# Nine pairs with seven products in the second column pair of the down projection, sums in used-up channels, and the pairs in another order

## The chip, the cores and the metric

The kernel runs on one core of a Trainium2 chip. The metric is the device time of one execution in microseconds; the number to predict is the median of several. The engines are PE (matmul), DVE (element by element), ACT (activation and casts), POOL, and SP, whose queue gives out the transfers (DMA). They run at once and wait for each other by semaphores. Each works through its own instructions in a fixed order.

## The reference

One decoder layer on 256 tokens and 16 meta tokens, width 2048: an attention group and a gated delta group side by side, an output projection, a residual, and then a SwiGLU FFN of width 5632. The change lies in the FFN, most of it in its last product:

```python
u = rmsnorm(h, ffn_norm_w[l])
h = h + (jax.nn.silu(u @ w_gate[l]) * (u @ w_up[l])) @ w_down[l]
```

Everything is float32, and the weights are read from memory once.

## The kernel before, in words

**Products in parts.** PE multiplies a faster 32-bit form with fewer bits. So each weight tile (2 x 128 rows by 512 columns, 512 KB, named raw) is split: ACT casts it to hi (L274), DVE takes lo = raw - hi (L275). The other operand is split too, and a product is three matmuls, hi by hi, lo by hi and hi by lo. A matmul makes 128 x 512 outputs in one of eight banks, two rings of four, mm and aux.

**The stream of weights.** Before anything runs, a list gives the weight tiles in the order of use (order) and the forms that they are split into (forms). Raw tiles have 4 buffers (WR), split ones 6 (WS and WS2). SP's queue issues the loads in the order of the list; a load into a buffer waits until DVE and ACT are done with the tile that was there, and what stands behind it in the queue waits too. next_w() hands out the next split tile and has those up to six further on split. The order of ACT and SP is that of the program. The order of DVE and PE is chosen by a scheduler when the program is built.

**Pairs with seven products.** The FFN's work is cut into pairs: two 128-channel rows of the weights (k, k+1) by two column tiles by two halves of the tokens (b), eight products of 128 x 128 by 128 x 512. A pair in SEVEN (the up and gate chunks) or DSEVEN (down) takes seven products instead, by sums of its four blocks. Its weights come as four forms: g (first column tile, as it is), u (half of the second), and t and s, sums of the two that DVE makes (L291 to L294). An ordinary pair has two forms, 24 matmuls and two lo on DVE; one with seven has four forms, 21 matmuls, and on DVE four sums of 512 columns, three lo of 1024 and one of 512. The sums of the other operand (the "sides", side_forms, L1318 to L1330, on DVE and ACT) are made once for each pair and serve both halves of down. The seven products go to four banks of the other ring as well (y), and are added up later (down_mid, L1500 to L1504).

**Order of the FFN.** Chunk 0 of gate and up, by stream() (L1199), then chunks 1 to 10 by block() (L1381), then down as two blocks, one for each pair of its four column tiles (p = 0 and 1). A block goes through its 22 pairs in the order 0, 1, ..., 21. Side work (evictions, side sums, splits of the hidden state) runs as tasks that advance a step at each product, so that they are written into the program between the matmuls. ffn_task (L1298) makes chunk 0's hidden state, in gact, and hands it after "yield 2" to to_hT, which transposes it on PE (L1277) into a bank of mm. The seven sides of down are made at the start of block p = 0, together with the splits of the last three chunks (whole, L1466 and L1468). At the start of p = 1, the outputs of p = 0 are summed (L1504, L1516) and written (L1518), and the residual x1 for the next two column tiles is fetched into the same buffers (fetch_x1, L1484).

Of the kernel before, what the change touches and what calls it, by code (L numbers as in the profile page):

```python
# [15 lines left out]
P = 128  # L16
D = 2048
KT = D // P
# [3 lines left out]
FFN = 5632  # L22
# [3 lines left out]
NCH = FFN // 512  # L26
# [5 lines left out]
WR, WS = 4, 4  # L32
WS2 = 2
WHOLE = 8
SEVEN = (2, 4, 6)
DSEVEN = (7, 9, 11, 13, 15, 17, 19)
PER_STEP = 2
SLOT = 4
WARM = 14
# [127 lines left out]
def layer(tc, xT, aw, x, w_in, w_ba, w_out, w_gate, w_up, w_down, cmask, dist, par, out):  # L167
# [21 lines left out]
    mm = Ring(mmp, "mm", 4, 512)  # L189
    tasks = Tasks(PER_STEP)  # L190
    aux = Ring(auxp, "aux", 4, 512, tasks.slot)
# [28 lines left out]
    wd_v = w_down.rearrange("(kt p) c -> p kt c", p=P)  # L220
    order = []
# [12 lines left out]
    def w_tile(wv, q, c):  # L234
        return wv[:, 2 * q:2 * q + 2, 512 * c:512 * (c + 1)], 2, 512
# [4 lines left out]
    forms = [("w", i) for i in range(len(order))]  # L240
    for c in range(1, NCH):
        for q in range(KT // 2):
            i = len(order)
            order += [w_tile(wv, q, c) for wv in (wg_v, wu_v)]
            forms += [("w", i), ("w", i + 1)] if q not in SEVEN else [("g", i), ("u", i), ("t", i), ("s", i)]
    for c in (0, 2):
        for q in range(FFN // P // 2):
            i = len(order)
            order += [w_tile(wd_v, q, c + j) for j in range(2)]
            forms += [("w", i), ("w", i + 1)] if q not in DSEVEN else [("g", i), ("u", i), ("t", i), ("s", i)]  # L250
    raws, ready, sums_ = {}, {}, {}

    pos = [0, 0, 0, 0]
# [127 lines left out]
    for k in range(KT):  # L381
        src, w = xr[k // 8][:, k % 8, :], aw_sb[:, k:k + 1]
# [870 lines left out]
    hT = {}  # L1253
# [18 lines left out]
    def to_hT(c, b, h_):  # L1272
# [7 lines left out]
        if c not in hT:  # L1280
# [3 lines left out]
            elif c < 7:  # L1284
                hT[c] = keep.tile([P, 2, 4, SEQ], F32R, tag=("v_c", "k_c", "q_c")[c - 4], name=n)
            elif c < WHOLE:
                hT[c] = fpool[0].tile([P, 2, 4, SEQ], F32R, tag=n, name=n)
            else:
                hT[c] = fpool[0].tile([P, 4, SEQ], F32, tag=n, name=n)
        bs = slice(P * b, P * (b + 1))  # L1290
        if c < WHOLE:
            S.copy(hT[c][:, 0, :, bs], pst)
# [6 lines left out]
    def ffn_task(c, b, pg, pu):  # L1299
        g_ = yield from fpool[1].get(512)  # L1300
        act(g_, pg, AF.Silu, scale=rr[:, b:b + 1])
        mm.free()
        yield at_least(f"up{c}", 1)
        yield 1
        ps = pu[b]
        V.scalar_tensor_tensor(g_, ps, rr[:, b:b + 1], g_, ALU.mult, ALU.mult)
        mm.free()
        yield 2
        yield from to_hT(c, b, g_)


# [2 lines left out]
    def side_forms(key, h, l, sh, sl):  # L1314

        v = yield from fpool[1].get(2, SEQ)
        w = yield from fpool[1].get(4, P)
        V.tensor_tensor(v, h, l, ALU.add)  # L1318
        a11, a21, a12, a22 = v[:, 0, 0:P], v[:, 0, P:SEQ], v[:, 1, 0:P], v[:, 1, P:SEQ]
        V.tensor_tensor(w[:, 0], a21, a22, ALU.add)  # L1320
        V.tensor_tensor(w[:, 1], w[:, 0], a11, ALU.subtract)
        V.tensor_tensor(w[:, 2], a11, a21, ALU.subtract)
        V.tensor_tensor(w[:, 3], a12, w[:, 1], ALU.subtract)
        yield 2
        h1, l1 = h[:, 0, P:SEQ], l[:, 0, P:SEQ]
        S.copy(h1, w[:, 0])
        S.copy(sh, w[:, 1:4])
        yield 1
        V.tensor_tensor(l1, w[:, 0], h1, ALU.subtract)
        V.tensor_tensor(sl, w[:, 1:4], sh, ALU.subtract)  # L1330
        fpool[1].free(2)
        sides[key] = [(h1, l1)] + [(sh[:, i], sl[:, i]) for i in range(3)]
        mark(f"side{key}")
# [30 lines left out]
        yield 10  # L1364
        yield from to_hT(c, b, h_)

    def block(c, name, nq, seven, lhs, need, mid, end):

        ring, other = rings[c % 2], rings[(c + 1) % 2]
        tasks.until(lambda: ring.live == 0)  # L1370
        x = [ring.now() for _ in range(4)]
        y = []
        n = nq - len(seven)
        left = {("x", i): 3 * (2 * n + (len(seven) if i < 3 else 0)) for i in range(4)}
        left.update({("y", i): 3 * len(seven) for i in range(4)})
        todo = dict(left)

        def product(bank, a, w):
            for l, r in ((a[0], w[0]), (a[0], w[1]), (a[1], w[0])):
                first, todo[bank] = todo[bank] == left[bank], todo[bank] - 1  # L1380
                PE.matmul((x if bank[0] == "x" else y)[bank[1]], l, r, start=first, stop=todo[bank] == 0)  # L1381

        for q in range(nq):
            k = 2 * q
            if need:
                tasks.until(need(k))
            if q not in seven:
                for col in range(2):
                    hi, lo = next_w()
                    for i in range(2):  # L1390
                        for b in range(2):
                            product(("x", 2 * col + b), lhs(k + i, b), (hi[:, i], lo[:, i]))
                            tasks.step()
                    if q == nq - 1:
                        end(col, x)
                continue
            if not y:
                tasks.until(lambda: other.live == 0)
                y += [other.now() for _ in range(4)]
            tasks.until(at_least(f"side{(name, q)}", 1))  # L1400
            s1, s2_, s3, s4 = sides[name, q]
            plan = (((("y", 0), lhs(k, 0), 0), (("x", 0), lhs(k + 1, 0), 1)), ((("x", 2), s4, 1),),
                    ((("y", 3), s1, 0), (("y", 2), s3, 1)), ((("y", 1), s2_, 0), (("x", 1), lhs(k + 1, 1), 1)))
            for part in plan:
                hi, lo = next_w()
                for bank, a, i in part:
                    product(bank, a, (hi[:, i], lo[:, i]))
                    tasks.step()
            if q == seven[-1]:
                mid(y)  # L1410

    def chunk(c):
        t = []

        def end(col, x):
            if col == 0:
                for b in range(2):
                    tasks.spawn(end_task(c, b, x, t), urgent=True)

        def mid(y):  # L1420
            tasks.until(lambda: fpool[1].live == 0)
            t.extend(fpool[1].now((512,)) for _ in range(4))
            S.copy(t[0], y[0])
            tasks.spawn(mid_task(c, y, t), delay=0, urgent=True)

        block(c, "u", KT // 2, SEVEN, lhs_u, None, mid, end)
        mark(f"up{c}")

    def keep_x1():
# [15 lines left out]
    pu += stream(range(KT - 4), lhs_u, last=False)  # L1445
    for i, q in enumerate(SEVEN):
        k = slice(2 * q, 2 * q + 2)
# [7 lines left out]
    def whole(c):  # L1455
# [3 lines left out]
        if c < NCH - 1:  # L1459
            if "hl" not in hT:  # L1460
                hT["hl"] = keep.tile([P, NCH - 1 - WHOLE, 2, 4, SEQ], F32R, tag="xa", bufs=2, name="hT_hl")
            hi, lo = (hT["hl"][:, c - WHOLE, i] for i in range(2))
        else:
# [11 lines left out]
    def fetch_x1(p):  # L1475

        for j in range(2):
            n = f"hT{WHOLE + j}"
            if p == 0:
# [7 lines left out]
    def lhs_h(kt, b):  # L1487
        t = hT[kt // 4]
        bs = slice(P * b, P * (b + 1))
        if kt // 4 < WHOLE:  # L1490
            return tuple(t[:, i, kt % 4, bs] for i in range(2))
# [17 lines left out]
    def down_end(p, b, c, ps):  # L1509
# [8 lines left out]
            nc.sync.dma_start(out=out[P * b:P * (b + 1), o:o + w], in_=r_)  # L1518
        rings[(NCH + p) % 2].free()

    def down_side(i, q):
        if i < len(SEVEN):
            sh, sl = side_tiles(i)
        else:
            if i == len(SEVEN):

                yield at_least(f"hT{NCH - 1}", 3)
                t = fpool[0].tile([P, 6 * P], F32R, tag=f"hT{NCH - 1}", name=f"side{q}")
            else:
                o = 8 * SEQ + 6 * P * (i - len(SEVEN) - 1)  # L1530
                t = rest[:, o:o + 6 * P]
            sh, sl = (t[:, 3 * P * j:3 * P * (j + 1)].rearrange("p (a b) -> p a b", b=P) for j in range(2))
        k = slice(2 * q % 4, 2 * q % 4 + 2)
        c = q // 2
        yield at_least(f"hT{c}", 2 if c < WHOLE else 3)
        h, l = (hT[c][:, 0], hT[c][:, 1]) if c < WHOLE else hT[c]
        yield from side_forms(("h", q), h[:, k, :], l[:, k, :], sh, sl)

    for c in range(WHOLE, NCH):
        tasks.spawn(whole(c), delay=24)  # L1540
    for i, q in enumerate(DSEVEN):
        tasks.spawn(down_side(i, q), delay=24)
    tasks.spawn(fetch_x1(0), delay=24)
    for p in range(2):
        def end(col, x):
            for b in range(2):
                tasks.spawn(down_end(p, b, col, x[2 * col + b]), urgent=True)

        def mid(y):
            tasks.until(lambda: fpool[1].live <= 1)  # L1550
            t = [fpool[1].now((512,)) for _ in range(3)]
            S.copy(t[0], y[0])
            tasks.spawn(down_mid(p, y, *t), delay=0, urgent=True)

        block(NCH + p, "h", FFN // P // 2, DSEVEN, lhs_h, need_h, mid, end)
        if p == 0:
            tasks.spawn(fetch_x1(1), delay=12)
    tasks.until(lambda: not tasks.list)
# [66 lines left out]
```

## Time and profile before

| | |
|---|---|
| median of 3 runs | 1222.2 us (1222.12 to 1224.43) |
| the profiled execution | 1224.38 us, span 1222.6 us |
| PE busy | 1209.2 us, 7316 matmuls |
| DVE, ACT busy | 983.6 and 692.3 us |
| raw tiles of down | 88 of 512 KB, 4.6 us from issue to landing in the median |
| read from memory | 221.83 MB, 186 GB/s over the span |

In the rows of the timeline stand the start in us from the span's beginning, the duration, the engine, the line and what is written from what; in square brackets the idle time of the engine before it, and what ended it. In a list of waits stand the total, the count and the longest. A chain of waits follows the work that ended last back in time. In the rows by windows stand each engine's busy time and count in the window, the granted clock of PE, the busy share of the DMA engines and GB/s.

### The profile page before, as it was taken

Reading aid. Unit: us, or ns where it says so; the run is one execution under the profiler, and the core shown is the slowest. Engines: PE = TensorE matmul, PEld = TensorE weight load, DVE = VectorE, ACT = ScalarE, POOL = GpSimd, SP = SyncE. Lnnn points to the kernel's source line nnn. Section 1 sums busy time; section 2 is a strip of 40 time slices with the busy share of each in tenths; the row PEclk is TensorE's granted clock in tenths of the full one; section 3 lists DMA queues with packets and bytes.
Section 4 is the critical chain, followed back from the end, with each engine's and each line's share of the span. In section 5 each row is a group of like instructions: output and inputs, shape, how many; then the busy total and the mean of one; then the engine's idle time right before and its main releaser. Section 6 shows DMA issues by size and latency. Waiting matters only on the chain.

```text
span 1222.6 us, 19223 instructions
## 1 busy us (share of the span) xinstructions
PE 1209.2 (99%) x7316; PEld 1060.0 (87%) x7316; DVE 983.6 (80%) x1573; ACT 692.3 (57%) x1087; POOL 6.1 (0%) x14
## 2 busy tenths in 40 slices
PE   9999999999999999999999999999999999999998
PEld 7999999999999988887888888888888888888876
DVE  7989974686676666668889988998998899886686
ACT  7674465275776665455555556555555665553552
POOL 0000000000000000000000000000000000000000
PEclk9999999999999999999999999999999999999999
DMA  8466564344544645685665665566566565567543
GB/s 293 124 207 195 145 187 121 112 124 145 172 140 139 229 162 178 191 277 167 196 206 186 195 218 190 192 204 217 166 208 216 187 211 197 201 225 276 181 164 133
DMA packets 151869, 228.54 MB, mean 187 GB/s; under 512 B 11736, under 2 KB 72672, under 8 KB 151264
## 3 DMA queue, kind: packets, MB, share of 16 engines
q1 hardware_dynamic: 151232, 226.78, 57.4%
q8 instruction: 57, 0.93, 0.3%
q10 hardware_dynamic: 544, 0.52, 0.1%
q14 instruction: 36, 0.29, 0.1%
HBM read 221.83 MB, written 5.45 MB: 186 GB/s over the span
## 4 chain that ended last, share of the span: by engine, by line
PE 85%; DVE 7%; DMA 4%; ACT 2%; issue 1%; SPq 0%; DVEq 0%; ACTq 0%
PE aux L1381 25%; PE mm L1152 23%; PE mm L1381 21%; PE mm L1199 10%; DVE lo L275 3%; DMA raw<-in_w_down_dram 3%; ACT hi L274 1%; PE aux L1100 1%; PE aux L1055 1%; DMA raw<-in_w_in_dram 0%; PE mm L1277 0%; DVE s L293 0%; DMA raw<-in_w_up_dram 0%; DVE r L581 0%; PE aux L1277 0%
## 5 line engine op out<-in xcount | busy, mean ns | idle before, releaser
L274 ACT CAST hi<-raw 128x1024 fp32r<-128x1024 f32 (+1 forms) x412 | 405.1, 996 | 325.0 <-PE mm L1152 93.3
L275 DVE TENSOR_TENSOR lo<-raw,hi 128x1024 fp32r<-128x1024 f32 (+1 forms) x412 | 470.6, 1153 | 141.6 <-ACT hi L274 139.1
L1152 PE MATMUL mm<-xh,hi 128*128 128x272 f32 (+2 forms) x896 | 258.4, 289 | 0.0
L1152 PE MATMUL mm<-xl,hi 128*128 128x272 f32 (+2 forms) x896 | 255.9, 286 | 0.9 <-DVE xl L384 0.6
L1152 PE MATMUL mm<-xh,lo 128*128 128x272 f32 (+2 forms) x896 | 255.0, 286 | 1.0 <-DVE lo L275 1.0
L1152 PEld LDWEIGHTS mm<-xl,hi 128*128 128x128 f32 x896 | 168.5, 188 | 2.2 <-DVE xl L384 2.0
L1152 PEld LDWEIGHTS mm<-xh,hi 128*128 128x128 f32 x896 | 168.6, 188 | 2.1 <-issue 1.5
L1152 PEld LDWEIGHTS mm<-xh,lo 128*128 128x128 f32 x896 | 168.2, 188 | 1.6 <-DVE lo L275 1.4
L1381 PE MATMUL aux<-hi,uh 128*128 128x512 f32 x260 | 101.6, 391 | 0.0
L1381 PE MATMUL mm<-hi,uh 128*128 128x512 f32 x260 | 101.6, 391 | 0.0
L1381 PE MATMUL aux<-hi,ul 128*128 128x512 f32 x260 | 101.3, 390 | 0.0
L1381 PE MATMUL mm<-hi,ul 128*128 128x512 f32 x260 | 101.2, 389 | 0.0
L1381 PE MATMUL aux<-lo,uh 128*128 128x512 f32 x260 | 101.2, 389 | 0.0
L1381 PE MATMUL mm<-lo,uh 128*128 128x512 f32 x260 | 101.2, 389 | 0.0
L1381 PE MATMUL aux<-hi,hT 128*128 128x512 f32 x216 | 70.2, 389 | 0.0
L1381 PE MATMUL mm<-hi,hT 128*128 128x512 f32 x216 | 70.0, 389 | 0.0
L274 ACT CAST hi<-s 128x1024 fp32r<-128x1024 f32 x44 | 46.3, 1053 | 38.0 <-DVE s L294 34.5
L291 DVE TENSOR_TENSOR t<-raw,raw 128x512 f32<-128x512 f32 x44 | 30.2, 687 | 38.7 <-DMA raw<-in_w_down_dram 25.2
L274 ACT CAST hi<-t 128x1024 fp32r<-128x1024 f32 x44 | 46.3, 1053 | 26.2 <-DVE t L292 11.3
L1381 PEld LDWEIGHTS aux<-hi,ul 128*128 128x128 f32 x260 | 48.8, 188 | 10.2
L1381 PEld LDWEIGHTS mm<-hi,ul 128*128 128x128 f32 x260 | 48.8, 188 | 10.2
L1381 PEld LDWEIGHTS mm<-hi,uh 128*128 128x128 f32 x260 | 48.8, 188 | 10.0
(418 smaller groups left out, 2046.8 us busy)
## 6 DMA issues: line engine op xcount, KB each, us to landing
raw<-in_w_in_dram SPq DMA_DIRECT2D x111, 512.0 KB, 3.6
raw<-in_w_gate_dram SPq DMA_DIRECT2D x88, 512.0 KB, 3.7
raw<-in_w_up_dram SPq DMA_DIRECT2D x88, 512.0 KB, 4.4
raw<-in_w_down_dram SPq DMA_DIRECT2D x88, 512.0 KB, 4.6
raw<-in_w_out_dram SPq DMA_DIRECT2D x32, 512.0 KB, 4.2
x<-x1d SPq DMA_DIRECT2D x8, 256.0 KB, 4.8
xr<-in_xT_dram SPq DMA_DIRECT2D x7, 272.0 KB, 5.8
out_dram<-x SPq DMA_DIRECT2D x6, 256.0 KB, 5.1
```

The lines of the kernel that those rows point to most:

```text
L274: S.copy(hi[:, js], raw[:, js])
L275: V.tensor_tensor(lo[:, js], raw[:, js], hi[:, js], ALU.subtract)
L291: V.tensor_tensor(t[:, 0], u[:, 0], g[:, 0], ALU.subtract)
L1055: PE.matmul(pss[m][:, cut[n]], q[ms, P * n:P * (n + 1)], k[ms, 0:NK[n]], start=True, stop=True)
L1100: PE.matmul(po[:, n, :], l, r, start=(j == 0), stop=(j == 1 + n))
L1152: PE.matmul(acc[c][:, 0:n], a[:, k, cs], b[:, kt, t0:T], start=(kt == 0 and i == 0), stop=(kt == KT - 1 and i == 2))
L1199: PE.matmul(acc[b], l, r[:, i % 2, :], start=(first and i == 0 and j == 0), stop=(last and i == len(kts) - 1 and j == 2))
L1381: PE.matmul((x if bank[0] == "x" else y)[bank[1]], l, r, start=first, stop=todo[bank] == 0)
```

## The change

Four edits. Block p = 1 of down has two more pairs with seven products, 3 and 5 (EXTRA), so nine. Their sides have no room of their own: they are put into hT[0], the channels of pairs 0 and 1, whose last products are over then; the tasks that make them are started after these two pairs of block p = 1 (past). The pairs of both blocks get a new order, written as two strings (ROWS): N stands for the next ordinary pair, S for the next one with seven. In p = 0 the pairs with seven stand at places 5, 7, 10, 12, 15, 17 and 19 (before: 7, 9, 11, 13, 15, 17, 19), in p = 1 at 2, 5, 7, 9, 11, 13, 15, 17 and 19, pairs 3 and 5 last; the loads follow the same order. And chunk 0's ffn_task waits 8 steps instead of 2 ahead of its transposes.

```diff
+ROWS = ("NNNNNSNSNNSNSNNSNSNSNN", "NNSNNSNSNSNSNSNSNSNSNN")
 SEVEN = (2, 4, 6)
 DSEVEN = (7, 9, 11, 13, 15, 17, 19)
+EXTRA = (3, 5)
...
-    for c in (0, 2):
-        for q in range(FFN // P // 2):
+    DSETS = (DSEVEN, DSEVEN + EXTRA)
+
+    def down_rows(p):
+        plain = iter(q for q in range(FFN // P // 2) if q not in DSETS[p])
+        seven = iter(DSETS[p])
+        return [next(plain if r == "N" else seven) for r in ROWS[p]]
+
+    for p in range(2):
+        for q in down_rows(p):
             i = len(order)
-            order += [w_tile(wd_v, q, c + j) for j in range(2)]
-            forms += [("w", i), ("w", i + 1)] if q not in DSEVEN else [("g", i), ("u", i), ("t", i), ("s", i)]
+            order += [w_tile(wd_v, q, 2 * p + j) for j in range(2)]
+            forms += [("w", i), ("w", i + 1)] if q not in DSETS[p] else [("g", i), ("u", i), ("t", i), ("s", i)]
...
-        yield 2
+        yield 8
         yield from to_hT(c, b, g_)
...
-        for q in range(nq):
+        for q in rows:
...
-                    if q == nq - 1:
+                    if q == rows[-1]:
                         end(col, x)
+                if past:
+                    past(q)
                 continue
...
+    def extra_side(q):
+
+        i = EXTRA.index(q)
+        sh, sl = (hT[i // 2][:, j, 2 * i % 4:2 * i % 4 + 2, :].rearrange("p a b -> p (a b)")[:, 0:3 * P]
+                  .rearrange("p (a b) -> p a b", b=P) for j in range(2))
+        k = slice(2 * q % 4, 2 * q % 4 + 2)
+        h = hT[q // 2]
+        yield from side_forms(("h", q), h[:, 0, k, :], h[:, 1, k, :], sh, sl)
+
...
-        block(NCH + p, "h", FFN // P // 2, DSEVEN, lhs_h, need_h, mid, end)
+        def past(q):
+            if p == 1 and q < len(EXTRA):
+                tasks.spawn(extra_side(EXTRA[q]), delay=12)
+
+        block(NCH + p, "h", down_rows(p), DSETS[p], lhs_h, need_h, mid, end, past)
```

More of the change, by code (lines that the diff above doesn't have):

```diff
@@ L1365, in end_task, with block @@
         yield from to_hT(c, b, h_)
-    def block(c, name, nq, seven, lhs, need, mid, end):
+    def block(c, name, rows, seven, lhs, need, mid, end, past=None):
         ring, other = rings[c % 2], rings[(c + 1) % 2]
@@ L1372, in block @@
         y = []
-        n = nq - len(seven)
+        n = len(rows) - len(seven)
         left = {("x", i): 3 * (2 * n + (len(seven) if i < 3 else 0)) for i in range(4)}
@@ L1424, in mid @@
             tasks.spawn(mid_task(c, y, t), delay=0, urgent=True)
-        block(c, "u", KT // 2, SEVEN, lhs_u, None, mid, end)
+        block(c, "u", range(KT // 2), SEVEN, lhs_u, None, mid, end)
         mark(f"up{c}")
```

## The prediction

> **What bounds it now.** I read the page first, then PE's waits over the whole run, then the chain of waits, then DVE, PE and SP by the timeline in the second half, and last the order in which the new program's instructions stand. Two names: an N row is one pair of weight tiles with eight products, an S row one with seven; "block 0" and "block 1" are down's two column pairs.
>
> ```profile
> PE 1209.2 (99%) x7316; PEld 1060.0 (87%) x7316; DVE 983.6 (80%) x1573; ACT 692.3 (57%) x1087; POOL 6.1 (0%) x14
> PE mm L1381 <- DVE lo L275: 3.3, 3, 1.8
> PE mm L1277 <- DVE gact L1306: 1.3, 1, 1.3
> ```
>
> PE is busy in 1209.2 of 1222.6 us. Of its waits after the first product of the FFN there are two: 1.3 us on gact (start of chunk 1) and 3.3 us on lo (three times, all in block 1, below). Everything else is set by the count of matmuls, so work saved on PE is gained one to one, and any new wait of PE is paid one to one.
>
> ```profile
> 992.46 29.95 PE aux L1381 x132
> 1024.45 2.04 PE mm L1381 x9
> 1034.65 2.04 PE mm L1381 x9
> ```
>
> These steps of the chain of waits give PE's pace: 29.95/132 = 0.227 us a matmul. An N row is 24 matmuls, 5.44 us; an S row 21, 4.76 us; N and S together 10.20 us, which is also the distance of the two x9 steps (the last nine matmuls that an S row puts into the other ring; nine others go ahead of them). So block 0's first S row, row 7, starts at 1024.45 - 2.04 = 1022.4, and the block at 1022.4 - 7 x 5.44 = 984.3.
>
> **What the change removes.** (1) Two more S rows save three matmuls each: 6 x 0.227 = 1.4 us. The order of PE has 6367 rows against 6373, so this is done.
>
> (2) "yield 8" puts the eight transposes of chunk 0 later on PE. Of PE, at the start of chunk 1, before:
>
> ```order
> L1381 MATMUL aux_6787<-hi_6674,ul 128x512
> L1277 MATMUL mm_6813<-ident,gact_6609 128x128 x4
> L1381 MATMUL aux_6788<-hi_6674,uh 128x512
> L1381 MATMUL aux_6788<-lo_6675,uh 128x512
> L1277 MATMUL mm_6818<-ident,gact_6612 128x128 x4
> ```
>
> and now:
>
> ```order
> L1391 MATMUL aux_6786<-hi_6692,uh 128x512
> L1391 MATMUL aux_6786<-lo_6693,uh 128x512
> L1391 MATMUL aux_6786<-hi_6692,ul 128x512
> L1287 MATMUL mm_6841<-ident,gact_6609 128x128 x4
> L1287 MATMUL mm_6846<-ident,gact_6612 128x128 x4
> ```
>
> They stood behind 21 matmuls of the chunk and stand behind 30.
>
> ```profile
> 557.83 0.39 PE L1381 MATMUL aux<-hi,uh 128*128 128x512 f32 x1
> 564.08 0.66 PE L1277 MATMUL mm<-ident,gact 128*128 128x128 f32 x4 [1.34 <-DVE gact L1306]
> 564.15 0.74 DVE L1306 SCALAR_TENSOR_TENSOR gact<-mm,rr,gact 128x512 f32<-128x512 f32 x1
> ```
>
> 30 matmuls from 557.83 end at 564.6, when the first gact is there and the second 0.3 us off: the 1.34 us go, and what follows (lo of the chunk's first S row) is not later. Gain 1.3 (0 if the hT copies behind the transposes become late, as the S row there needs their bank).
>
> **What it adds in block 0.** The S rows move from 7, 9, ... to 5, 7, 10, 12, ... Row 5's S starts at 984.3 + 27.2 = 1011.5, row 6 at 1016.3, and row 6's second tile is due at 1016.3 + 12 x 0.227 = 1019.0. In these 30 us DVE also makes the side sums, and has no room:
>
> ```profile
> 992.00:1022.00 30.00, 30.00 (x136) 24.90 (x135) 29.10 (x65) 16.30 (x28) 0.00 (x0) 1.00 0.57 188
> 989.93 2.35 DVE L275 TENSOR_TENSOR lo<-raw,hi 128x1024 fp32r<-128x1024 f32 x2
> 996.27 0.69 DVE L1318 TENSOR_TENSOR gact<-hT 128x512 f32<-128x512 f32 x1
> 1007.46 0.28 DVE L1329 TENSOR_TENSOR hT<-gact,hT 128x128 fp32r<-128x128 f32 x1
> 1007.66 0.55 DVE L1330 TENSOR_TENSOR sl<-gact,sh 128x384 fp32r<-128x384 f32 x1
> 1008.13 0.28 DVE L1329 TENSOR_TENSOR hT<-gact,hT 128x128 fp32r<-128x128 f32 x1
> 1016.72 0.68 DVE L291 TENSOR_TENSOR t<-raw,raw 128x512 f32<-128x512 f32 x1
> 1017.32 0.68 DVE L292 TENSOR_TENSOR t<-raw 128x512 f32<-128x512 f32 x1
> 1025.15 3.49 DVE L275 TENSOR_TENSOR lo<-raw,hi 128x1024 fp32r<-128x1024 f32 x3
> ```
>
> Busy 29.1 of 30. From start to start: 0.20 us for 128 columns, 0.47 for 384, 0.60 for 512, and 3.49/3 = about 1.14 for 1024. Of DVE, where row 6 of block 0 is split, before (lo_10565 and lo_10608 are the low parts of its two tiles):
>
> ```order
> L275 TENSOR_TENSOR lo_10565<-raw_10487,hi_10564 128x1024
> L1329 TENSOR_TENSOR hT_7952<-gact_10547,hT_7952 128x128
> L1330 TENSOR_TENSOR sl_10537<-gact_10547,sh_10536 128x384
> L1329 TENSOR_TENSOR hT_8310<-gact_10558,hT_8310 128x128
> L1330 TENSOR_TENSOR sl_10539<-gact_10558,sh_10538 128x384
> L1320 TENSOR_TENSOR gact_10601<-gact_10600 128x128
> L1322 TENSOR_TENSOR gact_10601<-gact_10600 128x128
> L1321 TENSOR_TENSOR gact_10601<-gact_10601,gact_10600 128x128
> L275 TENSOR_TENSOR lo_10608<-raw_10505,hi_10607 128x1024
> ```
>
> and now (lo_10695 is the low part of the second tile; the first's stands 13 rows ahead of it):
>
> ```order
> L1330 TENSOR_TENSOR gact_10661<-gact_10660 128x128
> L1332 TENSOR_TENSOR gact_10661<-gact_10660 128x128
> L1331 TENSOR_TENSOR gact_10661<-gact_10661,gact_10660 128x128
> L1340 TENSOR_TENSOR rest<-gact_10645,rest 128x384
> L1333 TENSOR_TENSOR gact_10661<-gact_10660,gact_10661 128x128
> L1339 TENSOR_TENSOR hT_hl<-gact_10661,hT_hl 128x128
> L301 TENSOR_TENSOR t_10710<-raw_10655,raw_10529 128x512
> L1340 TENSOR_TENSOR rest<-gact_10661,rest 128x384
> L302 TENSOR_TENSOR t_10710<-raw_10655 128x512
> L285 TENSOR_TENSOR lo_10695<-raw_10527,hi_10694 128x1024
> ```
>
> All seven sides and row 5's four sums now stand ahead of row 6. Up to the row that starts at 996.27 before, the two orders are the same; from there to lo_10695 the new one has 9 instructions of 1024 columns, 12 of 512, 7 of 384 and 28 of 128: 10.3 + 7.2 + 3.3 + 5.6 = 26.4 us, so 1022.6 at the earliest. Its first row, t of row 5, waits for a tile whose buffer comes free at 992.28:
>
> ```profile
> raw<-in_w_down_dram SPq DMA_DIRECT2D x88, 512.0 KB, 4.6
> ```
>
> With 4.6 us to landing that is a wait of 0.6; if two transfers share, 1.7. With 1.1 for it and 0.6 for results used at once, lo_10695 ends at 1024.3. Behind it lie 10 + 19 matmuls up to the end of the S row 7, 6.6 us: 1030.9, against 1011.5 + 4.8 + 5.4 + 4.8 = 1026.5. Stall 4.4 us (2.7 with no wait, 5.4 with 1.7 and another 0.4 on ACT, whose casts stand in the same order). After it two N rows follow, DVE catches up, and I see no later wait in block 0: no more than two S rows come close together. ACT and PE wait behind this DVE row, nobody else.
>
> **What it adds in block 1.** Here S rows stand at 2, 5, 7, ... 19. Call lead the time from L291 of an S row (it starts when the row's second tile lands) to PE's start of that row.
>
> ```profile
> 1055.84 0.69 DVE L291 TENSOR_TENSOR t<-raw,raw 128x512 f32<-128x512 f32 x1 [1.22 <-DMA raw<-in_w_down_dram]
> 1065.95 0.69 DVE L291 TENSOR_TENSOR t<-raw,raw 128x512 f32<-128x512 f32 x1 [1.17 <-DMA raw<-in_w_down_dram]
> 1076.72 0.69 DVE L291 TENSOR_TENSOR t<-raw,raw 128x512 f32<-128x512 f32 x1 [2.00 <-DMA raw<-in_w_down_dram]
> 1150.09 0.69 DVE L291 TENSOR_TENSOR t<-raw,raw 128x512 f32<-128x512 f32 x1 [2.93 <-DMA raw<-in_w_down_dram]
> 1157.57 0.39 PE L1381 MATMUL aux<-hi,hT 128*128 128x512 f32 x1
> 1161.23 0.69 DVE L291 TENSOR_TENSOR t<-raw,raw 128x512 f32<-128x512 f32 x1 [2.36 <-DMA raw<-in_w_down_dram]
> 1176.17 0.50 PE L1381 MATMUL mm<-lo,hT 128*128 128x512 f32 x1 [0.53 <-DVE lo L275]
> 1187.64 0.50 PE L1381 MATMUL mm<-lo,hT_hl 128*128 128x512 f32 x1 [0.93 <-DVE lo L275]
> 1196.84 0.69 DVE L291 TENSOR_TENSOR t<-raw,raw 128x512 f32<-128x512 f32 x1 [3.51 <-DMA raw<-in_w_down_dram]
> 1199.93 0.50 PE L1381 MATMUL mm<-lo,hT_hl 128*128 128x512 f32 x1 [1.79 <-DVE lo L275]
> 1202.57 0.39 PE L1381 MATMUL aux<-hi,hT_hl 128*128 128x512 f32 x1
> ```
>
> Row 11's lead is 1157.57 - 1150.09 = 7.5, row 19's 1202.57 - 1196.84 = 5.7. The loop from one L291 to the next (sums, lo, buffer free, DMA, landing) takes (1196.84 - 1150.09)/4 = 11.7 us here, 10.1 and 10.8 at the end of block 0, against PE's 10.20. At a lead of 5.7 PE waits, since the lo of the N row's second tile stands behind L293. From row 11 to 19 PE took 45.0 us where 40.8 were due: 4.2 lost.
>
> ```profile
> 1107.42 4.26 SPq L1484 DMA_DIRECT2D x<-x1d  x4
> 1111.74 90.87 SPq L261 DMA_DIRECT2D raw<-in_w_down_dram  x33
> ```
>
> Now the lead runs out sooner. SP's queue stands on the output writes and the x1 fetches until 1111.74, 12.6 after block 1's start B (984.3 + 15 x 5.44 + 7 x 4.76 = 1099.2); row 2's sums now stand on DVE ahead of what those writes wait for, four of 0.6 us, so it is free at B + 15. Row 5's second tile lands some 6.5 later with two others and the fetches, B + 22; two lo come first, then 3.7 us of sums and sides until its buffer is free, B + 27.7; row 7's lands 5 later, B + 32.7, and PE is due there at B + 36.7: lead 4.0, when before the first two S rows had more than 12. Then six periods to row 19, three near 11.2 (the lo's order there frees a buffer sooner) and three at 11.7: 68.7 against 61.2, 7.5 lost, and 1.7 more to bring the lead from 4.0 to 5.7: 9.2, against 4.2. Cost 5.0 us. With block 0's last loops (10.45) it is 1.5 + 1.7 - 4.2 = -1; with 12.2, the slowest, 12 + 1.7 - 4.2 = 9.5. I take 11.2 to 11.7, since block 1's own rows are nearest. The two more side sums (2.6 us of DVE each) lie in rows 2 to 5 and are in the 3.7; if DVE were free there they would cost nothing. What follows row 19 (two N rows, the last sums, the output) is as it was.
>
> **Sum.** -1.4 - 1.3 + 4.4 + 5.0 = +6.7 us. On the profiled execution's 1224.4 that is 1231.1; the median shown is 1222.2, so I say 1228.9. The measurement tells about 0.2% (2.4 us) from no change.
>
> **Rivals.** *The stalls are covered* (0.12): DVE works ahead enough, loops run near 10.4, and the savings stand with block 1 a little better: 1222.2 - 2.7 = 1219.5. For it speaks that PE never waited from 984 to 1150; against it the count of DVE's rows. *One block stalls, the other not* (0.20): 1222.2 - 2.7 + 4.4 or 5.0 = 1224 to 1224.5, on the edge of no change. *PE goes cold* (0.06): while row 6 waits, PE would idle over 2 us in one piece, and restart at the pace it has at the program's start:
>
> ```profile
> PEclk9999999999999999999999999999999999999999
> ```
>
> ```profile
> 1.20 4.83 PE L324 MATMUL aux<-zero 128*128 128x512 bf16 x14 [1.20 <-DVE zero L321]
> ```
>
> The granted clock reads 9 in all 40 slices, but the 14 matmuls there take 0.345 us each against 0.227: 14 x 0.12 = 1.7 us more, 1230.6. After the 1.79 us of idle at 1199.93 nothing of the kind shows (the eleven matmuls up to 1202.57 take 0.24 each), so it decides only for longer gaps. The Trainium skill's "TensorE: Matmul & The Clock Gate", section "HAM oscillation", puts the limit at idle gaps over some 3.4 us; by it the clock stays up here, and no run shows a gap that long.
>
> The likeliest, both blocks stall, has 0.62. Slower by over 0.2%: 0.62 + 0.06 + half of 0.20 = 0.78, less 0.03 for small stalls: 0.75; within 0.2%: 0.13; faster: 0.12. Range: below, small stalls in both, -2.7 + 2.7 - 1 = -1, 1221; above, 5.4 + 9.5 - 2.7 = +12.2, 1234.5.
>
> **What would show it.** Right: PE's waits list lo L285 with one or two gaps over 1 us near 1015 to 1024 and five or six in block 1 from row 5 on; the wait on gact is gone; L301 in block 1 comes every 11 us or more. Wrong: no PE gap in block 0, or a loop near 10.2.

## The result and the profile after

The changed kernel takes 1233.0 us in the median of 4 executions (1230.14 to 1235.44), the kernel before 1222.45 beside it (1222.12 to 1224.43): slower, ratio 1.0075 with a 95% interval of 1.0055 to 1.0096. The forecast was 1228.9 us in a range of 1221.0 to 1234.5, with 0.75 for slower. The profiled execution of after is the lowest of the four, 1230.14 us.

The page of after, its span and the busy times:

```profile
span 1228.4 us, 19245 instructions
PE 1210.9 (99%) x7310; PEld 1058.2 (86%) x7310; DVE 996.1 (81%) x1599; ACT 695.7 (57%) x1095; POOL 6.1 (0%) x14
```

PE has six matmuls less (7310 for 7316) and is yet busy 1.7 us longer as the page counts it (among others because a matmul that starts after a wait has a row of 0.50 us, others 0.39); the span is 5.8 us longer. So the time lies in and around waits. The list of PE's waits in after, the rows that belong to down:

```profile
PE mm L1391 <- DVE lo L285: 4.8, 6, 1.4
PE aux L1391 <- ACT hi L284: 2.4, 2, 1.4
PE aux L1391 <- DVE lo L285: 1.3, 3, 1.0
PE mm L1391 <- ACT hi L284: 0.2, 1, 0.2
```

8.7 us in twelve waits, where before had 3.3 in three. The row of 1.3 us on gact is gone. To say where time is lost, I count from now on what a block of down *loses*: the time from its first matmul to the next block's first, less 0.2267 us for each of its matmuls (10.20 us for the 45 of an N and an S row). In block 1, which has no next block, the time ends 0.2267 us after the last matmul's start. It holds waits, restarts after them, and matmuls at a slow clock.

| traced execution | block 0 starts | block 0 loses | block 1 loses | last matmul starts |
|---|---|---|---|---|
| before | 983.27 | 0.9 | 4.2 | 1217.99 |
| after | 981.80 | 5.8 | 7.9 | 1223.77 |

The 0.9 of block 0 are transposes in its row 1, in both. So: -1.5 ahead of block 0, +4.9 in block 0, +3.7 in block 1, -1.4 for six matmuls: +5.8, the difference of the spans.

Block 0's stall in the timeline of PE, after (row 5, an S row, starts at 1009.9):

```profile
1014.44 0.39 PE L1391 MATMUL aux<-hi,hT 128*128 128x512 f32 x1
1016.18 0.50 PE L1391 MATMUL aux<-hi,hT 128*128 128x512 f32 x1 [1.36 <-ACT hi L284]
1017.71 0.50 PE L1391 MATMUL aux<-lo,hT 128*128 128x512 f32 x1 [1.02 <-DVE lo L285]
1021.49 0.73 PE L1391 MATMUL aux<-hi,hT 128*128 128x512 f32 x2 [1.00 <-ACT hi L284]
1022.43 0.50 PE L1391 MATMUL mm<-hi,hT 128*128 128x512 f32 x1 [0.21 <-ACT hi L284]
```

Row 6's first tile is late, and its second again. What DVE and ACT did then, from their timelines in after:

```profile
1015.36 0.55 DVE L1340 TENSOR_TENSOR rest<-gact,rest 128x384 fp32r<-128x384 f32 x1
1016.44 1.22 DVE L285 TENSOR_TENSOR lo<-raw,hi 128x1024 fp32r<-128x1024 f32 x1
1020.06 0.69 DVE L301 TENSOR_TENSOR t<-raw,raw 128x512 f32<-128x512 f32 x1
1020.66 0.55 DVE L1340 TENSOR_TENSOR rest<-gact,rest 128x384 fp32r<-128x384 f32 x1
1021.73 2.35 DVE L285 TENSOR_TENSOR lo<-raw,hi 128x1024 fp32r<-128x1024 f32 x2
```

```profile
1011.31 0.30 ACT L1336 CAST hT<-gact 128x128 fp32r<-128x128 f32 x1 [4.87 <-DVE gact L1330]
1015.09 1.04 ACT L284 CAST hi<-raw 128x1024 fp32r<-128x1024 f32 x1
1019.97 0.51 ACT L1337 CAST rest<-gact 128x384 fp32r<-128x384 f32 x1 [0.78 <-DVE gact L1333]
1020.39 2.51 ACT L284 CAST hi<-raw 128x1024 fp32r<-128x1024 f32 x3
```

Row 6's two lo stand on DVE between the last sides, as the order said. And ACT, whose order is the program's, had been idle for 4.87 us waiting for a side's sum from DVE, while row 6's first tile had landed at 997.7 already: the cast that row 6 needs (1015.09) stands behind the casts of the sides. So PE waits for ACT by name, and ACT for DVE. The windows of after show DVE with no room:

```profile
1005.00:1015.00 10.00, 9.83 (x44) 7.81 (x42) 10.00 (x24) 2.88 (x7) 0.00 (x0) 1.00 0.43 149
1015.00:1025.00 10.00, 6.57 (x25) 4.42 (x26) 10.00 (x22) 6.13 (x10) 0.00 (x0) 1.00 0.23 75
```

(PE, PEld, DVE, ACT, POOL, then the granted clock, the DMA share and GB/s.) DVE is busy for all of both windows, the DMA for 0.23 of the second.

Block 1, the queue of SP at its start (B = 1102.5), and L301 of the rows 5, 7, 9 and 19:

```profile
1107.58 2.00 SPq L1530 DMA_DIRECT2D out_dram<-x  x2
1111.77 6.46 SPq L1496 DMA_DIRECT2D x<-x1d  x4
1118.33 13.39 SPq L271 DMA_DIRECT2D raw<-in_w_down_dram  x7
```

```profile
1127.56 0.68 DVE L301 TENSOR_TENSOR t<-raw,raw 128x512 f32<-128x512 f32 x1
1136.36 0.69 DVE L301 TENSOR_TENSOR t<-raw,raw 128x512 f32<-128x512 f32 x1 [0.96 <-DMA raw<-in_w_down_dram]
1147.29 0.69 DVE L301 TENSOR_TENSOR t<-raw,raw 128x512 f32<-128x512 f32 x1 [1.99 <-DMA raw<-in_w_down_dram]
1202.63 0.69 DVE L301 TENSOR_TENSOR t<-raw,raw 128x512 f32<-128x512 f32 x1 [2.40 <-DMA raw<-in_w_down_dram]
```

The queue is free at B + 15.8, and row 7 (PE starts it at 1141.04) has a lead of 4.7. From 1136.36 to 1202.63 the loop takes 66.27/6 = 11.05 us a period, PE's own pace being 10.20. PE waits for lo in row 5 and in every second row from 8 on but row 16; its first wait in row 5 and its longest, in row 14:

```profile
1131.38 0.50 PE L1391 MATMUL mm<-lo,sh 128*128 128x512 f32 x1 [0.62 <-DVE lo L285]
1183.97 0.50 PE L1391 MATMUL mm<-lo,hT 128*128 128x512 f32 x1 [1.41 <-DVE lo L285]
```

Of the 7.9 us, row 5 loses 1.8 and the rows from 7 to 19 lose 6.1.

### The profile page after: what moved, and what is told of

It reads as the page before. It is cut to its first block, busy times and chain, and to the rows that moved or that the text cites. A ratio compares the mean times of both kernels' runs of the same rounds, so it can differ in the third digit from the quotient of the medians.

```text
span 1228.4 us, 19245 instructions
## 1 busy us (share of the span) xinstructions
PE 1210.9 (99%) x7310; PEld 1058.2 (86%) x7310; DVE 996.1 (81%) x1599; ACT 695.7 (57%) x1095; POOL 6.1 (0%) x14
## 4 chain that ended last, share of the span: by engine, by line
PE 69%; DVE 16%; DMA 9%; ACT 3%; issue 2%; SPq 1%; DVEq 0%; ACTq 0%
PE mm L1162 19%; PE mm L1391 17%; PE aux L1391 16%; PE mm L1209 11%; DVE lo L285 7%; DMA raw<-in_w_down_dram 6%; ACT hi L284 2%; DVE r L591 1%; DVE s L303 1%; DMA raw<-in_w_in_dram 1%; PE aux L1110 1%; DVE t L301 1%; DVE s L304 1%; DVE t L302 1%; PE aux L1065 1%
## 5 line engine op out<-in xcount | busy, mean ns | idle before, releaser
L1391 PE MATMUL aux<-hi,hT 128*128 128x512 f32 x232 | 76.3, 391 | 2.4 <-ACT hi L284 2.4
L1391 PE MATMUL mm<-hi,hT 128*128 128x512 f32 x196 | 64.7, 390 | 0.2 <-ACT hi L284 0.2
L301 DVE TENSOR_TENSOR t<-raw,raw 128x512 f32<-128x512 f32 x46 | 31.7, 689 | 36.3 <-DMA raw<-in_w_down_dram 22.4
L1391 PEld LDWEIGHTS aux<-hi,ul 128*128 128x128 f32 x260 | 48.8, 188 | 10.2
L1391 PEld LDWEIGHTS aux<-lo,uh 128*128 128x128 f32 x260 | 48.8, 188 | 10.0
```

The source lines that it names most:

```text
L301: V.tensor_tensor(t[:, 0], u[:, 0], g[:, 0], ALU.subtract)
```

## The experiments

All have the changed kernel as their base but where it is said otherwise, and each ratio is to the kernel before, on the same chip. There its median was 1224.65 (experiments 1 to 4), 1224.75 (5 to 8), 1224.2 (9 to 11) and 1224.0 us (12). What the blocks lost is from the one traced execution of each.

| | block 0 | block 1 | block 0 loses | block 1 loses | ratio, 95% interval |
|---|---|---|---|---|---|
| 1 | old order | new, nine S | 0.9 | 8.5 | 1.0021 (1.0007 to 1.0034) |
| 2 | new order | old, seven S | 6.0 | 5.1 | 1.0047 (1.0030 to 1.0063) |
| 3 | old | old, seven S | 0.9 | 2.3 | 0.9998 (0.9986 to 1.0010) |
| 4 | new, late sides | new, nine S | 4.8 | 10.7 | 1.0053 (1.0034 to 1.0072) |
| 5 | old | seven S, spread | 0.9 | 0.3 | 0.9970 (0.9958 to 0.9983) |
| 6 | old | new, writes on POOL | 0.9 | 12.0 | 1.0045 (1.0028 to 1.0062) |
| 7 | old | spread, writes on POOL | 0.9 | 0.0 | 0.9974 (0.9963 to 0.9985) |
| 8 | old | old, writes on POOL | 0.9 | 3.2 | 0.9996 (0.9986 to 1.0007) |
| 9 | old | eight S, four in a run | 0.9 | 4.3 | 0.9997 (0.9983 to 1.0010) |
| 10 | new | new, nine S | 6.1 | 9.3 | 1.0075 (1.0058 to 1.0093) |
| 11 | new | seven S, spread | 6.3 | 1.7 | 1.0018 (1.0003 to 1.0033) |
| 12 | old | eight S, even | 0.9 | 1.5 | 0.9981 (0.9970 to 0.9993) |

**1. Block 0 in its old order.**

```diff
-ROWS = ("NNNNNSNSNNSNSNNSNSNSNN", "NNSNNSNSNSNSNSNSNSNSNN")
+ROWS = ("NNNNNNNSNSNSNSNSNSNSNN", "NNSNNSNSNSNSNSNSNSNSNN")
```

> Block 0 has its old order back (S rows at 7, 9, ... 19), the rest is as in the changed kernel. Theory (two stalls of their own, block 0's from DVE's sides and sums ahead of row 6, block 1's from its buffer loop): block 0 loses 0.9 us again instead of 5.8, block 1 still 7.9, so the profiled execution takes 1230.1 - 4.9 = 1225.3 us; the clock, below 1.000 in three of the four executions of the changed kernel, drops because of block 0's gaps, so it reads 1.000 and the median lies at 1225 too, 8 us under the changed kernel's. Rival 1 (the clock drops because of block 1's gaps): the median stays 2 to 4 us above the best execution, 1228. Rival 2 (the lost time only moves, since one buffer loop sets both blocks): block 1 loses 10 us or more, 1229.

Ratio 1.0021, +2.6 us, where the theory had 1225.3 - 1222.4 = +2.9; the trace has block 0 back at 0.9 and block 1 at 8.5. PE's waits from 980 us on:

```profile
PE mm L1391 <- DVE lo L285: 5.4, 7, 1.2
PE aux L1391 <- DVE lo L285: 0.2, 1, 0.2
```

No wait on ACT's hi is left. The two stalls are of their own: nothing moved over to block 1. Rival 2 falls. Rival 1 isn't told apart: the median lies 3.2 us over the best execution, but that of the kernel before does so by 4.2. The clock read 0.998 in 3 of 12 executions, 0.999 or 1.000 in the others.

**2. Block 1 in its old order, with its old seven S rows.**

```diff
-ROWS = ("NNNNNSNSNNSNSNNSNSNSNN", "NNSNNSNSNSNSNSNSNSNSNN")
+ROWS = ("NNNNNSNSNNSNSNNSNSNSNN", "NNNNNNNSNSNSNSNSNSNSNN")
-EXTRA = (3, 5)
+EXTRA = ()
```

> Block 1 has its old order and its old seven S rows back (six matmuls more, 1.4 us), block 0 keeps the new order. Theory: block 0 loses 5.8 us as in the changed kernel, block 1 4.2 as in the kernel before: the profiled execution takes 1230.1 - 3.7 + 1.4 = 1227.8 us, and if block 0's gaps are what lowers the clock, the clock reads 0.997 to 0.998 in most executions and the median is near 1230. Rival 1 (block 1's gaps lower it): 1.000 throughout, median 1227.8. Rival 2 (the loss only moves): block 1 loses 7 or more, 1231 with the clock up.

Ratio 1.0047, +5.8 us: block 0 loses 6.0 and block 1 5.1, between the theory's 4.2 and rival 2's 7. The clock read 0.998 or less in 3 of 10 executions, not in most. Either block's edit alone makes the kernel slower.

**3. The kernel before, with nothing but the later transposes.**

```diff
-        yield 2
+        yield 8
```

> The kernel before with nothing but the later transposes of gact (a yield of 8 for 2). Theory: the wait on gact goes, 1.3 to 1.5 us: 1221.0 us, clock 1.000. Rival (the wait is replaced, by a lo or a bank that comes late): 1222.4, no change, with a new wait in chunk 1.

Ratio 0.9998: not told apart from nothing, and the interval of 1.7 us down to 1.2 up holds the 1.4 expected as well. The trace has the wait on gact gone (the eight transposes go through in one piece), and PE is 1.6 us further at chunk 1's first products in each traced kernel with this edit, counted from one and the same matmul at 550 us. The time is hidden by something ahead of the FFN that differs by more (below, unexpected).

**4. The sides of the last five S rows begun later.**

```diff
-        tasks.spawn(down_side(i, q), delay=24)
+        tasks.spawn(down_side(i, q), delay=24 if i < 2 else 68 + 16 * (i - 2))
```

> The changed kernel, but the sides of the last five S rows are begun 40 to 100 products later, so that four of the seven no longer stand ahead of row 6 of block 0 on DVE. Theory (these sides make row 6's lo late): about 9 us of DVE go from ahead of it, block 0 loses 0.9 to 2.4 us instead of 5.8, the profiled execution takes 1225 to 1227 us, and the clock stays at 1.000. Rival 1 (the raw buffers and transfers of the S rows 5 and 7 set it): block 0 still loses 5 us or more, 1230. Rival 2 (the sides hit a later row instead): the gaps at row 6 go, others of 1 us or more appear at rows 9 to 19 of block 0, 1228 to 1231.

The gaps at row 6 are gone, as the theory says, and come back at rows 11, 12, 16 and 18 (1.5, 0.6, 0.3 and 1.5 us) and at row 5 of block 1 (4.0): rival 2. DVE had 130.0 us of work from 985 to 1135 us in this trace and in that of after. So the sides make row 6 late, but putting them later is no cure: in this one other placement DVE had as much to do and was late at other rows. This trace also caught the clock falling; the timeline of PE and windows of 2 us in block 1, row 5:

```profile
1133.92 0.50 PE L1391 MATMUL mm<-lo,sh 128*128 128x512 f32 x1 [1.65 <-DVE lo L285]
1135.85 0.63 PE L1391 MATMUL aux<-hi,sh 128*128 128x512 f32 x1
1136.27 0.63 PE L1391 MATMUL aux<-lo,sh 128*128 128x512 f32 x1
```

```profile
1134.00:1136.00 2.00, 1.83 (x6) 1.18 (x7) 2.00 (x4) 2.00 (x3) 0.00 (x0) 0.83 0.79 257
1136.00:1138.00 2.00, 2.00 (x7) 1.51 (x6) 1.94 (x2) 0.81 (x1) 0.00 (x0) 0.50 0.69 251
1138.00:1140.00 2.00, 2.00 (x9) 1.61 (x8) 1.05 (x2) 0.85 (x2) 0.00 (x0) 0.81 0.43 118
```

After a wait of 1.65 us the granted clock is 0.50 for 3.4 us, and a matmul takes 0.43 us from start to start instead of 0.23: eight of them, 1.6 us lost on top of the wait.

**5. Block 0 old, block 1 with seven S rows spread.**

```diff
+ROWS = ("NNNNNNNSNSNSNSNSNSNSNN", "NNSNNSNNSNNSNNSNNSNSNN")
+EXTRA = ()
```

> Block 0 in its old order, block 1 with seven S rows at 2, 5, 8, 11, 14, 17, 19, mostly two N rows between them; the later transposes of gact stay. Theory (in block 1 the loop of four buffers turns two rows in 10.6 to 11.9 us, so an S row every 10.2 us of PE's time loses, one every 15.6 does not): row 5 still loses the 1.8 us that SP's queue costs, rows 8 to 16 lose nothing, 18 at most 1; block 1 loses 2 to 3 us, against 4.2 of the kernel before and 8.5 of the run with block 0's old order alone. With 1.4 for gact that is 2.6 to 3.6 under the kernel before, 0.2 to 0.3%. Rival (every S row costs about 1 us wherever it stands, by the order of lo and sums on DVE): seven times 0.9 to 1.2, 6 to 8 us, 1 to 3 us slower than the kernel before.

Ratio 0.9970, 1220.4 us against 1224.75: faster than both kernels. Block 1 loses 0.3 where 2 to 3 were expected, and PE has no wait at all there that the profile lists. L301 of the rows 8, 11, 14 and 17 in this trace:

```profile
1138.99 0.69 DVE L301 TENSOR_TENSOR t<-raw,raw 128x512 f32<-128x512 f32 x1 [0.73 <-DMA raw<-in_w_down_dram]
1152.26 0.69 DVE L301 TENSOR_TENSOR t<-raw,raw 128x512 f32<-128x512 f32 x1 [0.56 <-DMA raw<-in_w_down_dram]
1165.10 0.69 DVE L301 TENSOR_TENSOR t<-raw,raw 128x512 f32<-128x512 f32 x1
1180.86 0.69 DVE L301 TENSOR_TENSOR t<-raw,raw 128x512 f32<-128x512 f32 x1
```

PE starts these rows at 1143.3, 1158.9, 1174.6 and 1190.2: leads of 4.3, 6.6, 9.5 and 9.3. With two N rows between, three rows come round in 13.3 and 12.8 us, PE needs 15.6, and lead is gained until the buffers are full. The rival (each S row costs a microsecond) falls.

**6. The output writes and the fetches of x1 from POOL, in experiment 1's kernel.**

```diff
-                nc.sync.dma_start(out=t[:, b], in_=x1d[b][:, cs])
+                nc.gpsimd.dma_start(out=t[:, b], in_=x1d[b][:, cs])
...
-            nc.sync.dma_start(out=out[P * b:P * (b + 1), o:o + w], in_=r_)
+            nc.gpsimd.dma_start(out=out[P * b:P * (b + 1), o:o + w], in_=r_)
```

> Block 0 in its old order, block 1 in the changed order with nine S rows, and the output writes and the fetches of x1 go out from GpSimd instead of SyncE, so that the loads of w_down no longer stand behind them. Theory (SP's queue, held for 11 us at the start of block 1, takes the lead at rows 5 and 7): the loads go on through 1103 to 1114, row 5 loses nothing instead of 1.8, row 7's lead is 8 us or more instead of 4.7, and at 0.5 to 1 us lost of it in each pair of rows block 1 loses 0 to 4 us instead of 8.5: 4 to 8 us under the run with block 0's old order alone, 0.1 to 0.4% under the kernel before. Rival 1 (the lead is short because four buffers cannot run ahead, whatever the queue does): block 1 loses 7 to 8.5 again. Rival 2 (issuing from GpSimd holds the ports of VectorE or takes long): sums and lo take longer, block 1 loses 8 or more.

Ratio 1.0045, not faster than experiment 1 (1.0021) but slower. SP's queue is held no more; the timeline of SP and windows of PE in this trace:

```profile
1085.70 47.77 SPq L271 DMA_DIRECT2D raw<-in_w_down_dram  x16
```

```profile
1134.00:1137.00 3.00, 3.00 (x8) 2.34 (x7) 2.96 (x4) 1.88 (x2) 0.00 (x0) 0.50 0.54 175
1161.00:1164.00 3.00, 3.00 (x9) 2.29 (x8) 3.00 (x5) 1.99 (x2) 0.00 (x0) 0.52 0.66 186
```

Row 5 lost 0.7 instead of 1.8, and rows 6 and 10 then 4.0 and 4.1, each a gap over 2 us and half clock behind it (1.7 each). Without those two 1.7 it is 8.6, what experiment 1 lost. Row 7's lead is 8.9 as the theory had it, but only because PE had lost 4.7 at rows 5 and 6 by then. Rival 1 holds: the queue decides where the first gap is, not how much is lost by row 19. My theory on the queue falls. So does rival 2: in block 1 a lo of 1024 columns took 1.22 us and a sum 0.69 in both experiments.

**7 and 8. The same edit with the spread order, and with the old orders.**

> Both edits: S rows of block 1 at 2, 5, 8, 11, 14, 17, 19 (seven), and the output writes and the fetches of x1 from GpSimd. Theory: nothing is left to wait for but the transposes of block 0's row 1: block 1 loses 0 to 1 us, 4.6 to 5.6 us under the kernel before, 0.4%. Rival (as for the two alone): 5 us or more lost in block 1, no faster than the kernel before.

> Both blocks in the old order with seven S rows each, the later transposes of gact, and the output writes and the fetches of x1 from GpSimd. Theory (the first S row of the old block 1 comes 38 us after its start, when SP's queue has long caught up): nothing but the 1.4 us of gact and a late transposes' wait of 0 to 0.5; block 1 loses 3 to 5 us as before; 0 to 0.15% under the kernel before. Rival (the held queue costs lead there too): block 1 loses under 1.5, 0.3% under.

0.9974 and 0.9996: with the spread order block 1 loses nothing in the trace, and yet the time isn't told apart from experiment 5's 0.9970; with the old order it is as the theory says, no difference.

**9. Block 1 with eight S rows, the last five (11, 13, ... 19) with one N row between.**

```diff
+ROWS = ("NNNNNNNSNSNSNSNSNSNSNN", "NNSNNSNNSNNSNSNSNSNSNN")
+EXTRA = (3,)
```

> Block 0 in its old order; block 1 with eight S rows (pair 3 the added one) at 2, 5, 8, 11, 13, 15, 17, 19. Theory (spacing, not number, is what costs): the leads gained by row 11 last for most of the four S rows that follow every second row: block 1 loses 0.3 at row 5 and 0 to 1.5 at rows 14 to 18, and three matmuls less save 0.7: 1219.5 to 1221.5, level with the run of seven spread S rows within 1 us, 0.25 to 0.4% under the kernel before. Rival (an eighth S row with its side is too much for VectorE): block 1 loses 3 or more, 2 us slower than the seven.

0.9997, and 4.3 us lost: the numbers of the rival, not mine. I had counted on leads gained by row 11; the lead there was 1158.0 - 1153.1 = 4.9, since up to there the stretches with two N rows had hardly begun to give back. Rows 12 to 18 then lose 0.5, 0.9, 1.1 and 1.7. Whether the eighth S row or the run of five costs was open; experiment 12 tells.

**10. The changed kernel once more.**

> The changed kernel once more, beside the others on one chip. Theory (two blocks' stalls, 5.8 less 1.5 for gact at the same clock, and a clock that falls to half for 3.4 us after some of the gaps): ratio 1.005 to 1.0075, clocks of 0.997 to 0.998 in most executions. Rival (the first four executions were high by chance): ratio 1.003 to 1.005.

1233.8 us, ratio 1.0075 (1.0058 to 1.0093): the first number again, not chance. But this trace has block 0 at 6.1 and block 1 at 9.3, where the first had 5.8 and 7.9: the first trace was one with small stalls. In this one the clock also fell to 0.50 inside block 0's stall, from 1019.9 to 1023.3 us. The clock read 0.997 in 2 of 6 executions, 0.999 or 1.000 in the rest, so "in most executions" was wrong.

**11. Block 0 new, block 1 spread.**

```diff
+ROWS = ("NNNNNSNSNNSNSNNSNSNSNN", "NNSNNSNNSNNSNNSNNSNSNN")
+EXTRA = ()
```

> Block 0 in the new order, block 1 with seven spread S rows. Theory (block 0's cost stands by itself): block 0 loses 5.8 to 6.0 in the trace, block 1 0 to 0.5; 4.9 to 5.1 us over the run with the old block 0 and the same block 1, or up to 7 where the clock falls too: 1225 to 1227.5. Rival (block 0's late end gives block 1's loads a lead, so that part comes back): under 4 us over it.

1.0018, against 0.9970 with the old block 0: 0.0048, 5.9 us for block 0's edit; by the traces 5.4 in block 0 and 1.4 more in block 1. PE's waits in down, two of 1.26 and 1.02 us at rows 5 and 6 as in after, the rest 0.4 to 0.7 each in block 0's row 18 and block 1's rows 4 and 5:

```profile
PE aux L1391 <- DVE lo L285: 1.8, 3, 1.0
PE aux L1391 <- ACT hi L284: 1.3, 1, 1.3
PE mm L1391 <- DVE lo L285: 0.7, 1, 0.7
```

Here the clock fell inside block 0's stall (0.50 at 1019 to 1021 us) and the rows 5 and 6 together lose 4.7, as in after (4.8); in experiment 10, with the same fall, they lose 5.2, in experiment 2, without, 5.1. Where PE waits for DVE anyway, a slow clock costs nothing that shows.

**12. Block 1 with eight S rows spread evenly.**

```diff
+ROWS = ("NNNNNNNSNSNSNSNSNSNSNN", "NNSNSNNSNSNNSNSNNSNSNN")
+EXTRA = (3,)
```

> Block 0 in its old order; block 1 with eight S rows (pair 3 the added one) spread evenly, by two and by one N row in turn, at 2, 4, 7, 9, 12, 14, 17, 19. Theory (it is the runs of S rows with one N row between that cost, since the loop of four buffers then takes 11 us or more for PE's 10.2, while a stretch with two N rows gives 2 to 3 us of lead back): each loss of 1 us is given back by the next stretch; block 1 loses 0 to 1.5 us (row 4 or 7 once, from the short start), 4.3 with the four S rows in a run at the end; 0.2 to 0.4% under the kernel before, 2 to 3.5 us under the run with eight S rows in the other order. Rival (the eighth S row itself, its sums and its side, is what VectorE cannot take): block 1 loses 3 us or more again, no faster than the kernel before.

0.9981, 1220.8 against 1224.0, and the trace has the shortest span of all, 1217.2 us. Block 1 loses 1.5, all of it at row 4. L301 of the rows 12, 14, 17 and 19:

```profile
1154.39 0.69 DVE L301 TENSOR_TENSOR t<-raw,raw 128x512 f32<-128x512 f32 x1
1162.13 0.69 DVE L301 TENSOR_TENSOR t<-raw,raw 128x512 f32<-128x512 f32 x1 [2.22 <-DMA raw<-in_w_down_dram]
1179.27 0.68 DVE L301 TENSOR_TENSOR t<-raw,raw 128x512 f32<-128x512 f32 x1
1187.78 0.69 DVE L301 TENSOR_TENSOR t<-raw,raw 128x512 f32<-128x512 f32 x1 [2.99 <-DMA raw<-in_w_down_dram]
```

PE starts them at 1161.2, 1171.4, 1187.0 and 1197.2: leads of 6.8, 9.3, 7.8 and 9.5, not short again after row 4 (1.0). As many S rows as in experiment 9, with the same sums and side: it is the run of them that costs, not the eighth. In time the two intervals overlap a little (0.9983 to 1.0010 there); the traces carry this verdict. Experiments 5, 7 and 12 lie within each other's intervals; which is best is not settled.

## Why the prediction was right, point by point

- **Six matmuls, -1.4**: -1.36 in the trace. Right.
- **The wait on gact, -1.3**: -1.5 ahead of block 0 in the trace of after, and -1.6 counted from one and the same matmul in every trace with the edit. Right there; experiment 3 can't tell it from zero by the time.
- **Block 0, +4.4 (2.7 to 5.4)**: +4.9 in the first trace, 5.1, 5.2 and 5.4 in those of 2, 10 and 11, and 5.9 us in time (11 against 5). The step held: row 6's two lo stand behind the sides, PE waits there and, but for 0.4 us at row 18 in the trace of 11, nowhere later in block 0. Row 6's second lo started at 1021.73 and, at 1.14 for one of the two in the row, ended at 1022.9; predicted was 1024.3, which is 1022.8 when block 0's earlier start (1.5) is taken off. Two things were sized too small: the wait for the landing was 1.5 us (1.1 taken), and ACT, for which I allowed 0.4 at most, held up row 6's first tile, because its casts keep the program's order and those of the sides wait for DVE. 2.6 of PE's waits in after go by ACT's name, all in block 0.
- **Block 1, +5.0 (-1 to +9.5)**: +3.7 in the first trace. In the new order the block lost 7.9, 8.5 and 9.3 (after, 1, 10), in the old order 4.2, 2.3 and 3.2 behind an old block 0 (before, 3, 8): 8.6 against 3.2 on average, +5.3. The steps: queue free at B + 15 (15.8), lead of row 7 4.0 (4.7; 1141.04 - 1136.36), loop 11.2 to 11.7 (11.05 here, 11.4 in experiment 10). Row 5 was later than I had it, L301 at B + 25, and lost 1.8, which I hadn't foreseen; that row 7's lead came out near 4.0 is luck, since without these 1.8 it would have been 2.9. From row 7 to 19 the terms were 7.5 for the loop and 1.7 for the lead; measured are 66.27 - 61.2 (six times 10.20) = 5.1 and, the lead going from 4.7 to 5.7, 1.0. What failed is the reason given for the short lead, the queue of SP: without it (6) the block loses as much. What decides is that in block 1 S rows with a single N row between come round in 11 us or more and PE wants them every 10.2 (9 against 12). The spacing is not the whole of it: in block 0 of the kernel before, the same tight order of seven came round in (1076.72 - 1016.72)/6 = 10.0 us and lost nothing. What makes the loop longer in block 1 no run here takes apart.
- **Sum, +6.7**: by the averages above -1.4 - 1.5 + 5.2 (block 0 by the traces of after, 2, 10 and 11) + 5.3 = +7.6 us; measured +9.2 by the ratio (6.7 to 11.7), +10.6 by the two medians and +9.6 in experiment 10. The profiled execution was forecast at 1231.1 us and took 1230.1, but it is the lowest of its four: the first trace's +5.8 is small because its block 1 was. What is left between 7.6 and 9.2 is inside the interval, and its cause is not shown.
- **The signs**: the wait on gact is gone, and PE has three gaps of 1 us or more between 1016 and 1022 us, but two of them go by ACT's hi and one by lo, where I had named lo alone. In block 1 PE waits in six rows, as said. L301 there comes every 11.05 us on average, but three of the six periods are under 11 (10.5, 10.6 and 10.9).
- **PE goes cold (0.06)** was underrated as an event: I had a single gap of 1.79 us with nothing behind it to go by, and the clock fell in row 6's stall in two of the four traces with the new block 0 (10 and 11). But the price of 1.7 us did not show there (11 above). The Trainium skill, "TensorE: Matmul & The Clock Gate", section "HAM oscillation", names PE gaps over some 3.4 us; by that rule the clock stays up. The runs disagree: the clock halved after gaps of 1.47, 1.65, 2.05, 2.06 and 2.20 us. It is not needed to make the changed kernel slow, since its first profiled execution has no such stretch in down and is slower by its waits alone; whether it adds to the slower executions is open.

## What to carry to other kernels

Where a kind of step is costly for an engine that works ahead, count its lead over the bound engine step by step: lead is lost in a run of such steps and gained back between them, so spread them evenly and let none come before the work ahead of them is through. A step that saves the bound engine 0.7 us is worth nothing if its supplier then comes round slower than the bound engine does: nine S rows in a tight order lose, eight spread evenly win against the kernel before, if not against seven spread. And when one engine's order is fixed by the program, look for what it casts or copies for others ahead of the thing you need; PE's wait for ACT here was DVE's work.

## What the runs showed that was not expected

**The clock falls after short gaps.** Half clock for 3.4 us, 1.6 to 1.7 us lost. In the traces, gaps of 1.47 (4, at 152.7 us), 1.65 (4), 2.05 (5, at 152.6), 2.06 and 2.20 (6) were followed by it, and so were 1.26 and 1.02 close together (11) and 1.72 and 1.02 (10). Gaps of 1.36, 1.02 and 1.00 close together and of 1.41 (after), of 1.61 and 1.03 close together (2), of 1.61 (10), 1.79 (before and 8), 1.84 (8), 1.88 (2) and 1.93 (3) were not.

The length of a gap does not sort these, but its place may. In each of the fourteen traces all changes of the clock lie whole multiples of 3.413 us apart (27.3 us, 8.0 times, in experiment 6; 979.6 us, 287.0 times, in experiment 4), so they stand on a fixed grid. In down, the stretches of this grid in which PE was idle for 1.82 us or more (1.82 in 4, 2.05 and 2.20 in 6, 1.87 in 10, 2.29 in 11) were each followed by half clock, and none with 1.79 or less was; the three gaps of after at row 6 lie in three stretches. At 152 us, among matmuls of 32x32, this does not hold: 1.47 and 2.05 us were followed by it, 1.84 was not. These are counts from few traces; no run here tests where the limit is. The Trainium skill, "TensorE: Matmul & The Clock Gate", section "Part 1: The HAM clock gate", tells of a free-running window of this length; the changes of the clock in these traces agree.

In experiment 2 the executions with a mean clock of 1.000, 0.999, 0.998 and 0.996 took 1227.8, 1229.9, 1232.5 and 1234.5 us on average (3, 4, 2 and 1 of them), and the four of after go the same way, 1230.1 at 1.000 and 1235.4 at 0.997. In the kernel before the slope comes and goes: 1224.5 at 1.000 and 1224.9 at 0.998 (11 and 4 executions beside experiments 1 to 4), but 1223.5 and 1227.1 (9 and 3 beside experiments 9 to 11). Whether the clock itself or the longer gaps ahead of it make that slope is open.

**Where executions of one program differ.** Most of the traces part between 150 and 166 us, long before anything that the change touches, and stay apart to the FFN: at one and the same matmul there, up to 3.4 us lie between them (5 against 12). In experiment 4 PE waits there where after does not:

```profile
154.12 0.72 PE L740 MATMUL aux<-r,gm 32*32 32x16 f32 x64 [1.47 <-DVE r L719]
```

and the clock is at 0.50 from 156 to 159 us. In after the same instruction starts at 152.35 with no wait. The executions of the kernel before spread over 6 us on one chip (1220.42 to 1226.63), so single executions say little on an edit of 1.4 us.
